# Modulation vectors of a hybrid encoder layer: VectorE's products with the condition vector taken by output channel, 2048 columns multiplied and summed in one operation, in place of 512-wide scaled additions

## The chip, the core and the metric

The kernel runs on one core of one Trainium2 chip. The metric is device microseconds from start to end of one execution. A core has five engines: TensorE (PE, matrix products into PSUM), VectorE (DVE), ScalarE (ACT), GpSimd (POOL) and SyncE (SP, which here only issues transfers). Sixteen DMA engines move data between device memory and the on-chip memory of 128 partitions.

## The reference, cut to what matters

```python
mod = jax.nn.silu(c) @ ada_w + ada_b          # c (1, 2048), ada_w (2048, 6 * 2048)
sh_m, sc_m, g_m, sh_f, sc_f, g_f = jnp.split((mod + ada_table[layer])[:, None, :], 6, axis=-1)
h = _rms(x, norm_mix_pre) * (1 + sc_m) + sh_m
y = _rwkv7_mix(h, ...)                          # 512 tokens, 2048 channels, 32 heads of 64
x = x + g_m * _rms(y, norm_mix_post)
h = _rms(x, norm_ffn_pre) * (1 + sc_f) + sh_f
f = _conv_ffn(h, ...)                           # hidden width 5504
x = x + g_f * _rms(f, norm_ffn_post)
```

Everything is float32. `silu(c) @ ada_w` is a product of one vector with a 2048 x 12288 matrix, 16 MB for each of the six modulation vectors. The change is about four of them, numbered as in the code: 2 is `g_m`, 3 is `sh_f`, 4 is `sc_f`, 5 is `g_f`.

## The kernel before, in words

Activations lie channel by token: 16 tiles of 128 channels (`KT` = 16) by 512 tokens. Every large product is taken in three matmuls of a split of both operands into a high and a low part (`mm3`, L265 to L267). Weights come in chunks of eight 128 x 128 blocks (`w_load`, L207, three buffers `wr`, on SP's queue). `w_split` halves a chunk: ACT writes the high part `wh` (L220), then VectorE the low part `wl` by a subtraction (L222), with four buffers each. So one half-chunk feeds four calls of `mm3`, which is 12 matmuls.

Each `mm3` calls `tick()`, which advances every generator in the list `sides` by one step. Work beside the products (the modulation vectors among it) is written as such generators and so is spread over the products; a number called pace says how many ticks lie between two jobs. The framework's scheduler then orders each engine's instructions by a simulation of the program; `behind()` tells it to put an operation after the last `wl`.

Vectors 0 and 1 are made by matmuls in the first stage (L361). Vectors 2 to 5 are made by `ada_jobs`. It goes over quarters of 512 output columns, and in a quarter over the 16 blocks of 128 input channels: a 128 x 512 tile of the matrix (`js`, or `xt` where six spare tiles are used) is loaded on SP (L458, 256 KB), and VectorE adds it, scaled by the 128 values of silu(c) for that block, to a running sum `ja` (L482; L477 for the first). After 16 blocks each partition holds a partial sum, so `finish` lets PE sum over the partitions by four matmuls with a column of ones (L464, which the profile counts as eight, two passes each), and VectorE adds the bias (L466). PE takes its queue in order, so what is queued behind L464 waits until the last `ja` is there.

Four stretches hold these jobs. `sc_f` (16 quarters x 16 blocks / 4 = 64 jobs) runs in the v products, with two buffers. Five of the eight quarters of `g_m` and `sh_f` run on POOL in the scan stage. The last three (48 jobs) run in the first output product `wo`, with six buffers `xt`. `g_f` (64 jobs) runs at the start of the last product `fo`, with three buffers. VectorE has 176 of the 256 jobs, or 11 of the 16 quarters.

Of the kernel before, what the change touches and what calls it, by code (L numbers as in the profile page):

```python
# [10 lines left out]
F32 = mybir.dt.float32  # L11
F32R = mybir.dt.float32r
AF = mybir.ActivationFunctionType
ALU = mybir.AluOpType

T = 512
# [14 lines left out]
         "mu0", "mu1", "mu2", "mu3", "mu4", "mu5", "w0", "a0", "kk", "ka", "rk", "lnw", "lnb", "c"]  # L31
VI = {n: i for i, n in enumerate(VEC_D)}


# [120 lines left out]
def body(ctx, tc, g, ap):  # L155
# [286 lines left out]
    QC = min(512, D)  # L442
    QB = QC // P

    def all_of(*vis):
        return [(vi, q) for vi in vis for q in range(D // QC)]

    def ada_jobs(pool, parts, bk, pace, bufs, eng=V, sums=1, get=None, last=False, to="ja"):
# [5 lines left out]
        def load(i):  # L454
            if i < len(todo):
                vi, q, k = todo[i]
                got[i] = get(i % bufs) if get else pool.tile([P, QC], F32, tag="js", name="js", bufs=bufs)
                nc.sync.dma_start(got[i], ap["ada2"][vi - 2, q, :, k])  # L458

# [35 lines left out]
        yield from finish()  # L495


    vp_stack = ExitStack()
# [27 lines left out]
    sides.append(xrest)  # L526
    jobs = ada_jobs(vp, all_of(4), 7, (1, 1, 1, 2), 2)
    vouts = [v_out(vbank[j], j) for j in range(nv0)]
# [465 lines left out]
    opened, jobs = [], []  # L994
    on_pool = len(all_of(2, 3)) * 5 // 8

    def begin():
        while fixed in sides or inv[0] in sides:
            yield
        ld_a[0], ld_b[0] = load_a(0), load_b(0)  # L1000
        for i, hv in enumerate(HV):
            nc.sync.dma_start(LH[i][hv, :, HD - i * HD:P - i * HD], d_bnd[0][hv, :, 2 - 2 * i])
        while s1_last in sides:
            yield
        invert_ready(KT)
        ss_stack.close()
        pool_of[0] = ss_stack.enter_context(tc.tile_pool(name="scn2", bufs=1))
        opened.append(True)
        wst["pool"] = 2
        ld_k[0] = load_k(0)  # L1010
        yield from solve(0)
        load_v(0, 0)
        load_v(0, 1)
        jobs.append(ada_jobs(pool_of[0], all_of(2, 3)[:on_pool], 2, (4,), 2, G, 2))
        sides.extend((s2_a, s2_b, jobs[0]))
# [66 lines left out]
    def spare(tag, name, w=T):  # L1082
        return ap_.tile([P, w], F32, tag=tag, name=name)
# [3 lines left out]
    def pair(tag, name):  # L1087
        t = ap_.tile([P, 2, T], F32, tag=tag, name=name)
        return [t[:, 0], t[:, 1]]
# [6 lines left out]
    acc1, accx = pair("b0", "acc")  # L1096
    xts = pair("b2", "xt") + pair("b3", "xt") + pair("b5", "xt")
    NX = len(xts)
    sqs = pair("b4", "osq")
# [63 lines left out]
    for b in range(KT - NL):  # L1163
        if b >= KT - NL - 4:
            fetch_x(*divmod(b - (KT - NL - 4), 2))
        ps = po[b] if b < n0 else kinner("wo", b, yx, bank((2, 6)[b % 2]))
        block_out(b, ps, acc1, yo[b], sqs[b % 2])
        if b == 1:
            jobs = ada_jobs(ap_, all_of(2, 3)[on_pool:], 7, (2,), NX, get=lambda i: xts[i], last=True, to="b1")
            sides.append(jobs)  # L1170
# [26 lines left out]
    def hidden(j, pg, pv):  # L1197
        if not units:
            units["g"], units["v"] = pair("b2", "ug"), spare("b3", "uv")
        ug = conv(pg, j, units["g"][j % 2])  # L1200
# [217 lines left out]
    ap_ = ctx.enter_context(tc.tile_pool(name="outp", bufs=1))  # L1418
    jobs = ada_jobs(ap_, all_of(5), 7, (2,), 3, last=True)
    sides.append(jobs)  # L1420
# [99 lines left out]
def layout(x):  # L1520
# [6 lines left out]
    for i, key in enumerate(g.units):  # L1527
# [9 lines left out]
    a["ada2"] = np.ascontiguousarray(  # L1537
        x["ada_w"].reshape(KT, P, 6, D // q, q)[:, :, 2:].transpose(2, 3, 1, 0, 4))
    cols = list(x["ada_b"].reshape(6, D)) + list(x["ada_table"][0].reshape(6, D))
# [23 lines left out]
```

## Time and profile before

| | us |
|---|---|
| three runs | 2730.96, 2741.63, 2741.87 (median 2741.63) |
| the profiled execution, its own time | 2733.9 |
| its span, first to last instruction | 2732.1 |
| PE busy | 2591.5 (95%) |
| VectorE busy | 2054.8 (75%) |
| ScalarE busy | 1332.1 (49%) |
| GpSimd busy | 811.5 (30%) |

The 1.8 us between the profiled execution's time and its span lie around the first and the last instruction. Busy times of engines overlap, and a busy engine is not always the one that others wait for; a row of a group gives its busy time, the mean of one instruction, and the idle time of the engine just before with what ended it.

### The profile page before, as it was taken

Reading aid. Unit: us, or ns where it says so; the run is one execution under the profiler, and the core shown is the slowest. Engines: PE = TensorE matmul, PEld = TensorE weight load, DVE = VectorE, ACT = ScalarE, POOL = GpSimd, SP = SyncE. Lnnn points to the kernel's source line nnn. Section 1 sums busy time; section 2 is a strip of 40 time slices with the busy share of each in tenths; the row PEclk is TensorE's granted clock in tenths of the full one; section 3 lists DMA queues with packets and bytes.
Section 4 is the critical chain, followed back from the end, with each engine's and each line's share of the span. In section 5 each row is a group of like instructions: output and inputs, shape, how many; then the busy total and the mean of one; then the engine's idle time right before and its main releaser. Section 6 shows DMA issues by size and latency. Waiting matters only on the chain.

```text
span 2732.1 us, 47677 instructions
## 1 busy us (share of the span) xinstructions
PE 2591.5 (95%) x17758; PEld 2277.4 (83%) x17758; DVE 2054.8 (75%) x3117; ACT 1332.1 (49%) x2313; POOL 811.5 (30%) x877
## 2 busy tenths in 40 slices
PE   5899999889999999999889999999999999999997
PEld 3568778667778787789789999999999988888896
DVE  6978588888677768668888788887888876644477
ACT  4442255454444445444665555555555553243464
POOL 3543013776878545401431111112121100000000
PEclk8999999999999999999999999999999999999998
DMA  8759776567776767477566767767767658623366
GB/s 307 281 194 347 240 252 216 193 196 237 207 175 189 198 170 195 127 269 237 187 198 195 198 194 192 205 190 201 197 192 205 175 184 283 205 94 101 99 201 206
DMA packets 301961, 555.59 MB, mean 203 GB/s; under 512 B 124352, under 2 KB 157504, under 8 KB 297632
## 3 DMA queue, kind: packets, MB, share of 16 engines
q1 hardware_dynamic: 271936, 441.05, 50.2%
q0 software_dynamic: 29360, 110.77, 15.4%
q8 instruction: 140, 2.29, 0.3%
q14 instruction: 93, 0.76, 0.1%
q10 hardware_dynamic: 432, 0.72, 0.1%
HBM read 474.18 MB, written 78.25 MB: 202 GB/s over the span
## 4 chain that ended last, share of the span: by engine, by line
PE 52%; DVE 4%; DMA 3%; issue 1%; ACT 1%; POOL 0%; DVEq 0%; ACTq 0%; POOLq 0%; SPq 0%
PE bk L1348 10%; PE bk L1347 10%; PE bk L1346 10%; PE bk L267 7%; PE bk L265 7%; PE bk L266 7%; DMA js<-ada 1%; DVE wl L222 1%; POOL acc L1137 0%; DVE fo L1443 0%; DVE yo L1128 0%; DMA x1t<-d_x 0%; PE bk L859 0%; DMA out<-x1t 0%; DVE ja L482 0%
## 5 line engine op out<-in xcount | busy, mean ns | idle before, releaser
L265 PE MATMUL bk<-xh,wh 128*128 128x512 f32 (+1 forms) x2204 | 779.1, 364 | 15.2 <-ACT wh L220 5.1
L266 PE MATMUL bk<-xl,wh 128*128 128x512 f32 (+1 forms) x2204 | 784.2, 360 | 1.9 <-DVE xl L1152 1.7
L267 PE MATMUL bk<-xh,wl 128*128 128x512 f32 (+1 forms) x2204 | 766.0, 362 | 15.7 <-DVE wl L222 15.2
L220 ACT CAST wh<-wr 128x512 fp32r<-128x512 f32 x584 | 357.5, 619 | 523.6 <-PE bk L266 446.9
L222 DVE TENSOR_TENSOR wl<-wr,wh 128x512 fp32r<-128x512 f32 x518 | 379.9, 739 | 210.5 <-ACT wh L220 191.5
L265 PEld LDWEIGHTS bk<-xh,wh 128*128 128x128 f32 x2204 | 419.8, 192 | 80.2 <-ACT wh L220 6.3
L267 PEld LDWEIGHTS bk<-xh,wl 128*128 128x128 f32 x2204 | 410.4, 192 | 83.8 <-DVE wl L222 23.2
L266 PEld LDWEIGHTS bk<-xl,wh 128*128 128x128 f32 x2204 | 421.2, 192 | 62.9 <-issue 3.0
L1297 POOL DMA_DIRECT2D ss<-w x78 | 68.0, 872 | 624.4 <-DMA ss<-w 386.1
L1347 PE MATMUL bk<-xl,wh 128*128 128x256 f32 x832 | 235.5, 283 | 0.0
L1348 PE MATMUL bk<-xh,wl 128*128 128x256 f32 x832 | 235.5, 283 | 0.0
L1346 PE MATMUL bk<-xh,wh 128*128 128x256 f32 x832 | 235.4, 283 | 0.0
L1346 PEld LDWEIGHTS bk<-xh,wh 128*128 128x128 f32 x832 | 159.7, 192 | 0.0
L1347 PEld LDWEIGHTS bk<-xl,wh 128*128 128x128 f32 x832 | 159.7, 192 | 0.0
L1348 PEld LDWEIGHTS bk<-xh,wl 128*128 128x128 f32 x832 | 159.7, 192 | 0.0
L1443 POOL TENSOR_TENSOR fo<-fo,rs 128x256 f32<-128x256 f32 x4 | 3.7, 914 | 489.3 <-ACT rs L1114 489.3
L482 DVE SCALAR_TENSOR_TENSOR ja<-js,cs,ja 128x512 f32<-128x512 f32 x120 | 89.8, 748 | 55.6 <-DMA js<-ada 54.7
L222 POOL TENSOR_TENSOR wl<-wr,wh 128x512 fp32r<-128x512 f32 x66 | 98.1, 1489 | 99.3 <-ACT wh L220 76.6
L1346 PE MATMUL bk<-xh,wx 128*128 128x256 f32 x416 | 117.7, 283 | 0.0
L1347 PE MATMUL bk<-xl,wx 128*128 128x256 f32 x416 | 117.7, 283 | 0.0
L1348 PE MATMUL bk<-xh,wx 128*128 128x256 f32 x416 | 117.7, 283 | 0.0
L1484 DVE TENSOR_TENSOR xl<-act,xh 128x512 fp32r<-128x512 f32 (+1 forms) x172 | 92.3, 552 | 27.0 <-ACT xh L1483 26.1
(302 smaller groups left out, 5962.8 us busy)
## 6 DMA issues: line engine op xcount, KB each, us to landing
wr<-w SPq DMA_DIRECT2D x370, 512.0 KB
js<-ada SPq DMA_DIRECT2D x208, 256.0 KB
ss<-w SPq DMA_DIRECT2D x78, 512.0 KB
ss<-w POOLq DMA_DIRECT2D x78, 512.0 KB, 8.2
ada<-ada SPq DMA_DIRECT2D x32, 1024.0 KB
w<-w SPq DMA_DIRECT2D x39, 512.0 KB
d_bnd<-bnd POOLq DMA_DIRECT2D x16, 768.0 KB, 4.1
d_gs<-big POOLq DMA_DIRECT2D x16, 768.0 KB, 4.6
```

Of the source, the lines that this page charges most:

```text
L220: S.copy(hi, r)
L222: ins = on.tensor_tensor(lo, r, hi.bitcast(F32), ALU.subtract)
L265: PE.matmul(out[:, cs], wh[0:kp, 0:m], xh[0:kp, cs], start=start, stop=False)
L266: PE.matmul(out[:, cs], wh[0:kp, 0:m], xl[0:kp, cs], start=False, stop=False)
L267: PE.matmul(out[:, cs], wl[0:kp, 0:m], xh[0:kp, cs], start=False, stop=stop)
L482: eng.scalar_tensor_tensor(a, w, c, a, ALU.mult, ALU.add)
L1297: G.dma_start(t[:, i], chunk(j, other), accum_op=ALU.add)
L1346: PE.matmul(ps, wh, xh, start=start and k == 0, stop=False, skip_group_check=True)
L1347: PE.matmul(ps, wh, xl, start=False, stop=False, skip_group_check=True)
L1348: PE.matmul(ps, wl, xh, start=False, stop=k == CH - 1, skip_group_check=True)
L1443: prev[of[kt]] = of[kt].tensor_tensor(fo[kt][:, cs], fo[kt][:, cs], rs4[:, cs], ALU.mult)
L1484: V.tensor_tensor(ahl[e][1][:, cs], act[f][:, cs], ahl[e][0][:, cs].bitcast(F32), ALU.subtract)
```

## The change

For VectorE's 11 quarters the matrix is laid out the other way: a tile `js` has 128 output channels on the partitions and the 2048 input channels along a row. silu(c) is written to device memory once (`d_c`) and read back as a row `crow` that is the same on all partitions. One operation multiplies the tile with that row and sums each partition's 2048 products into one column of `part`; a second one adds the bias. PE's sums are no longer needed for these quarters; POOL's five quarters stay as they were. 44 blocks of 128 channels take the place of 11 quarters: 16 for `sc_f`, 12 for `sh_f`, 16 for `g_f`. The last 16 are taken in two passes of 1024 columns, 32 operations, the second pass adding to the first's result. Buffers of `js`: two everywhere (1 MB each; 512 KB for `g_f`). Paces: 9 ticks a job for `sc_f`, 8 for `sh_f`, 5 for `g_f`.

```diff
-                nc.sync.dma_start(got[i], ap["ada2"][vi - 2, q, :, k])
+                nc.sync.dma_start(got[i], ap["ada2"][(vi - 2) * (D // QC) + q, :, k])
...
+    d_c = dram("d_c", (KT, P))
+    part = cp.tile([P, KT], F32, name="part")
+    def c_row(t, cols=slice(0, D)):
+        n = cols.stop - cols.start
+        nc.sync.dma_start(t, d_c.rearrange("k p -> (k p)")[cols].unsqueeze(0).to_broadcast([P, n]))
+        return t
+    def row_jobs(todo, crow, get, bufs, pace, cols=slice(0, D)):
+        got = {}
+        def load(i):
+            if i < len(todo):
+                got[i] = get(i % bufs)
+                nc.sync.dma_start(got[i], ap["ada3"][ROWS.index(todo[i])][:, cols])
+        for i in range(bufs):
+            load(i)
+        yield
+        for n, (vi, b) in enumerate(todo):
+            w, to = got.pop(n), part[:, b:b + 1]
+            with behind():
+                V.scalar_tensor_tensor(w, w, 1.0, crow, ALU.mult, ALU.mult, accum_out=to)
+            V.tensor_tensor(mods[vi][:, b:b + 1], to, mods[vi][:, b:b + 1] if cols.start else bt[:, vi, b:b + 1], ALU.add)
+            load(n + bufs)
+            for _ in range(pace):
+                yield
...
-    jobs = ada_jobs(vp, all_of(4), 7, (1, 1, 1, 2), 2)
+    nc.sync.dma_start(d_c.rearrange("k p -> p k"), cs)
+    crow = c_row(vp.tile([P, D], F32, name="crow"))
+    jobs = row_jobs([r for r in ROWS if r[0] == 4], crow, lambda i: vp.tile([P, D], F32, tag="js", name="js", bufs=2), 2, 9)
...
-            jobs = ada_jobs(ap_, all_of(2, 3)[on_pool:], 7, (2,), NX, get=lambda i: xts[i], last=True, to="b1")
+            jobs = row_jobs([r for r in ROWS if r[0] < 4], c_row(spare("b2", "crow", D)),
+                            lambda i: tp.tile([P, D], F32, tag=f"t3{'hl'[i]}", name="js"), 2, 8)
...
-            units["g"], units["v"] = pair("b2", "ug"), spare("b3", "uv")
+            t = ap_.tile([P, 4, T], F32, tag="b2", name="ug")
+            units["g"], units["v"] = [t[:, 0], t[:, 1]], t[:, 2]
...
-    jobs = ada_jobs(ap_, all_of(5), 7, (2,), 3, last=True)
+    def in_halves():
+        for cols in (slice(0, D // 2), slice(D // 2, D)):
+            row = c_row(ap_.tile([P, D // 2], F32, tag="crow", name="crow"), cols)
+            yield from row_jobs([r for r in ROWS if r[0] == 5], row,
+                                lambda i: ap_.tile([P, D // 2], F32, tag="js", name="js", bufs=2), 2, 5, cols)
+    jobs = in_halves()
...
+    a["ada3"] = np.ascontiguousarray(np.stack([x["ada_w"][:, vi * D + b * P:vi * D + (b + 1) * P].T for vi, b in row_blocks(D)]))
```

The lines move by 11 and more, so L222 of before is L233 of the changed kernel, L265 is L276, L207 is L218, L508 is L551. The first place is PE's queue at the end of the v products (`bk` is a bank of PSUM; L508 turns a block of v). Before:

```order
L266 MATMUL bk_3002<-xl,wh 128x512
L508 MATMUL bk_3013<-cst,vs 128x128 x4
L464 MATMUL bk_2730<-ones,ja 128x1 x4
L265 MATMUL bk_3003<-xh,wh 128x512
L266 MATMUL bk_3003<-xl,wh 128x512
```

and now:

```order
L277 MATMUL bk_2849<-xl,wh 128x512
L551 MATMUL bk_2860<-cst,vs 128x128 x4
L276 MATMUL bk_2850<-xh,wh 128x512
L277 MATMUL bk_2850<-xl,wh 128x512
L278 MATMUL bk_2850<-xh,wl 128x512
```

The four sums with `ones` are gone, and the products of the last two v blocks follow the turned block directly.

The second place is VectorE's queue in the `wo` stretch (L1107, now L1149, adds squares for a norm). Before, from one quarter's last additions to the next one's first:

```order
L482 SCALAR_TENSOR_TENSOR ja<-xt,cs,ja 128x512 x2
L222 TENSOR_TENSOR wl<-wr,wh 128x512 x3
L1107 TENSOR_TENSOR acc<-acc,osq 128x512
L222 TENSOR_TENSOR wl<-wr,wh 128x512
L477 TENSOR_SCALAR ja<-xt,cs 128x512
L466 TENSOR_TENSOR mod_87<-bk_11839,bt 128x4
L482 SCALAR_TENSOR_TENSOR ja<-xt,cs,ja 128x512 x3
L222 TENSOR_TENSOR wl<-wr,wh 128x512
L482 SCALAR_TENSOR_TENSOR ja<-xt,cs,ja 128x512 x2
```

and now, from the first of the twelve blocks on:

```order
L534 SCALAR_TENSOR_TENSOR js,part<-js,crow 128x2048 x2
L233 TENSOR_TENSOR wl<-wr,wh 128x512
L535 TENSOR_TENSOR mod_87<-part,bt 128x1
L233 TENSOR_TENSOR wl<-wr,wh 128x512
L535 TENSOR_TENSOR mod_87<-part,bt 128x1
L233 TENSOR_TENSOR wl<-wr,wh 128x512
L534 SCALAR_TENSOR_TENSOR js,part<-js,crow 128x2048
L1149 TENSOR_TENSOR acc<-acc,osq 128x512
L233 TENSOR_TENSOR wl<-wr,wh 128x512
```

One long operation stands where four to six short ones stood, with one or two `wl` between two of them. Between the first and the last long operation VectorE has, beside them: in the v products 34 `wl`, 20 of L521, 9 of L510 and 8 of L518; in the `wo` stretch 19 `wl` and 4 of L1107; in the `fo` stretch 39 `wl` and 35 `xl` (L1484).

The third place is SP's queue at the start of the `wo` stretch (`xin` is the layer's input, read again). Before:

```order
L207 DMA wr<-w 128x1024 x6
L1161 DMA xin<-xT 128x8x256 x4
L207 DMA wr<-w 128x1024 x2
L458 DMA xt<-ada 128x512 x8
L207 DMA wr<-w 128x1024
```

and now:

```order
L218 DMA wr<-w 128x1024 x6
L526 DMA js<-ada 128x2048 x2
L1203 DMA xin<-xT 128x8x256 x4
L218 DMA wr<-w 128x1024 x2
L516 DMA crow<-d_c 128x2048
L218 DMA wr<-w 128x1024 x2
L526 DMA js<-ada 128x2048 x2
```

Two 1 MB tiles now go ahead of `xin` and of two weight chunks, and the 1 MB row `crow` ahead of the next two. The write of `d_c` (2048 elements of 4 bytes) stands early in the first stage, behind the first three weight chunks and ahead of the fourth tile of vectors 0 and 1.

## Rows read from the trace of the kernel before

**Rows 1.** The page: span, and TensorE's busy time

```profile
span 2732.1 us, 47677 instructions
PE 2591.5 (95%) x17758; PEld 2277.4 (83%) x17758; DVE 2054.8 (75%) x3117; ACT 1332.1 (49%) x2313; POOL 811.5 (30%) x877
```

**Rows 2.** Busy time by stretch: v products, after a wait, `wo`, `fo`

```profile
core 0: us, PE busy (x) PEld busy (x) DVE busy (x) ACT busy (x) POOL busy (x), PEclk, DMA share, GB/s
200.00:260.00 60.00, 59.89 (x293) 50.27 (x292) 54.30 (x87) 15.18 (x26) 24.07 (x42) 1.00 0.98 353
260.00:327.00 67.00, 63.49 (x308) 53.13 (x306) 38.02 (x59) 14.86 (x25) 7.08 (x11) 1.00 0.75 253
327.00:332.00 5.00, 4.69 (x18) 3.98 (x19) 2.49 (x6) 1.68 (x3) 0.76 (x1) 0.66 0.89 308
1185.00:1260.00 75.00, 75.00 (x432) 66.34 (x431) 61.46 (x97) 32.10 (x61) 0.00 (x0) 1.00 0.86 293
2232.00:2375.00 143.00, 139.46 (x617) 115.09 (x618) 102.28 (x161) 54.66 (x92) 0.00 (x0) 0.98 0.82 281
```

**Rows 3.** Groups by line: the matmuls with ones

```profile
L464 PE MATMUL bk<-ones,ja 128*128 128x1 f32 x128 | 16.6, 241 | 6.1 <-DVE ja L482 5.6 <-DVE bv L849 0.4
```

**Rows 4.** TensorE in order of time, around one sum in the v products

```profile
start us, us, engine line op out<-in xcount [idle before <-releaser]
...
253.16 0.39 PE L265 MATMUL bk<-xh,wh 128*128 128x512 f32 x1
253.39 0.39 PE L266 MATMUL bk<-xl,wh 128*128 128x512 f32 x1
253.89 1.05 PE L464 MATMUL bk<-ones,ja 128*128 128x1 f32 x8
254.80 0.47 PE L267 MATMUL bk<-xh,wl 128*128 128x512 f32 x1
```

**Rows 5.** The same at the end of the v products

```profile
327.31 1.25 PE L464 MATMUL bk<-ones,ja 128*128 128x1 f32 x8 [3.82 <-DVE ja L482]
328.42 0.77 PE L265 MATMUL bk<-xh,wh 128*128 128x512 f32 x1
...
331.51 0.39 PE L266 MATMUL bk<-xl,wh 128*128 128x512 f32 x1
```

**Rows 6.** The same in the `fo` stretch

```profile
2344.11 0.39 PE L266 MATMUL bk<-xl,wh 128*128 128x512 f32 x1
2345.44 1.02 PE L464 MATMUL bk<-ones,ja 128*128 128x1 f32 x8 [0.95 <-DVE ja L482]
2346.33 0.48 PE L267 MATMUL bk<-xh,wl 128*128 128x512 f32 x1
```

**Rows 7.** VectorE's groups by line, shapes apart

```profile
L482 DVE SCALAR_TENSOR_TENSOR ja<-js,cs,ja 128x512 f32<-128x512 f32 x120 | 89.8, 748 | 55.6 <-DMA js<-ada 54.7
L1303 DVE TENSOR_TENSOR s<-ss,w 128x1024 f32<-128x1024 f32 x39 | 47.7, 1222 | 0.8
L663 DVE TENSOR_TENSOR_SCAN cs<-cst,sw 128x512 f32<-128x512 f32 x16 | 21.0, 1313 | 0.3
L374 DVE TENSOR_TENSOR shm<-bk,bt 128x1 f32<-128x1 f32 x16 | 2.4, 148 | 8.4 <-PE bk L373 8.4
```

**Rows 8.** VectorE in order of time, v products: two `wl`, then one L482

```profile
316.67 1.29 DVE L222 TENSOR_TENSOR wl<-wr,wh 128x512 fp32r<-128x512 f32 x2
317.89 0.75 DVE L482 SCALAR_TENSOR_TENSOR ja<-js,cs,ja 128x512 f32<-128x512 f32 x1
318.56 0.68 DVE L510 COPY vt<-bk 128x512 f32<-128x512 f32 x1
```

**Rows 9.** Waits: engine, line, waited for: total us, times, longest

```profile
ACT wh L220 <- PE bk L266: 446.9, 320, 4.7
...
PE bk L267 <- DVE wl L222: 15.2, 24, 1.9
```

**Rows 10.** SP in order of time at the start of the `wo` stretch

```profile
1170.68 5.29 SPq L1161 DMA_DIRECT2D xin<-xT  x4
1176.07 7.05 SPq L207 DMA_DIRECT2D wr<-w  x2
1184.32 6.38 SPq L458 DMA_DIRECT2D xt<-ada  x8
```

**Rows 11.** The page: the queue of SP's transfers, packets, MB, share of 16 engines

```profile
q1 hardware_dynamic: 271936, 441.05, 50.2%
```

**Rows 12.** Busy time by stretch early in the first stage

```profile
35.00:40.00 5.00, 3.84 (x9) 2.90 (x10) 3.00 (x4) 0.70 (x2) 0.56 (x1) 0.50 0.35 118
40.00:45.00 5.00, 4.68 (x34) 3.09 (x33) 0.26 (x3) 0.99 (x2) 0.12 (x1) 0.87 0.16 26
```

More of the change, by code (lines that the diff above doesn't have):

```diff
@@ L32, with on_pool, row_blocks @@
 VI = {n: i for i, n in enumerate(VEC_D)}
+def on_pool(d):
+    return d // min(512, d) * 2 * 5 // 8
+def row_blocks(d):
+    n = min(512, d) // P
+    return [(vi, b) for vi in range(2, 6) for b in range(d // P) if ((vi - 2) * (d // P) + b) // n >= on_pool(d)]
 class Cfg:
@@ L443, in body @@
     QB = QC // P
+    ROWS = row_blocks(D)
     def all_of(*vis):
@@ L994, in body @@
     opened, jobs = [], []
-    on_pool = len(all_of(2, 3)) * 5 // 8
     def begin():
@@ L1013, in begin @@
         load_v(0, 1)
-        jobs.append(ada_jobs(pool_of[0], all_of(2, 3)[:on_pool], 2, (4,), 2, G, 2))
+        jobs.append(ada_jobs(pool_of[0], [(g // (D // QC) + 2, g % (D // QC)) for g in range(on_pool(D))], 2, (4,), 2, G, 2))
         sides.extend((s2_a, s2_b, jobs[0]))
@@ L1096, in body @@
     acc1, accx = pair("b0", "acc")
-    xts = pair("b2", "xt") + pair("b3", "xt") + pair("b5", "xt")
-    NX = len(xts)
     sqs = pair("b4", "osq")
@@ L1537, in layout @@
     a["ada2"] = np.ascontiguousarray(
-        x["ada_w"].reshape(KT, P, 6, D // q, q)[:, :, 2:].transpose(2, 3, 1, 0, 4))
+        x["ada_w"].reshape(KT, P, 6, D // q, q)[:, :, 2:].transpose(2, 3, 1, 0, 4).reshape(-1, P, KT, q)[:on_pool(D)])
+    a["ada3"] = np.ascontiguousarray(np.stack([x["ada_w"][:, vi * D + b * P:vi * D + (b + 1) * P].T for vi, b in row_blocks(D)]))
     cols = list(x["ada_b"].reshape(6, D)) + list(x["ada_table"][0].reshape(6, D))
```

## The prediction

> **What bounds the kernel now.** I read the page first, then the busy times of the stretches in which the jobs run, then TensorE's timeline around each of its sums, and last VectorE's groups and the waits. On the page PE is busy for 2591.5 us of a span of 2732.1 [rows 1]. By stretch the reader is to see that PE is the bound just where the changed work lies: 59.89 of 60 us and 63.49 of 67 in the v products, 75.00 of 75 in `wo`, 139.46 of 143 in `fo` [rows 2]. There a microsecond taken from PE's queue is a microsecond off the end, and one taken from VectorE is worth nothing unless PE waits for it. VectorE is busy for 54.30 of 60 us, 38.02 of 67, 61.46 of 75 and 102.28 of 143: behind PE, but not far. PE waits for `wl` for 15.2 us in 24 pieces over the whole kernel, and ACT waits for PE 320 times before it can write the next `wh` [rows 9]: the split weights are ready early, and the four buffers hold it back. One matmul of 512 columns starts every 0.23 us [rows 4], so a half-chunk of 12 lasts 2.73 us, and two half-chunks ahead, about 5.5 us, is the delay of VectorE that PE does not feel.
>
> **What the change removes.** All gain must come from PE's sums with ones. The group has 128 instructions and 16.6 us of busy time [rows 3]; 11 of 16 quarters go, so 88 x 16.6 / 128 = 11.4 us. One sum in the timeline bears this out: matmuls start at 253.39 and, with the eight between, at 254.80, which is 1.41 us in place of 0.23 [rows 4]. With them go PE's waits for the last `ja`, 5.6 us [rows 3]: 3.82 at the end of the v products [rows 5], 0.95 in `fo` [rows 6], and the rest in one more like it. Behind the wait of 3.82 us PE is also slow: seven matmuls start from 328.42 to 331.51, 3.09 us in place of 7 x 0.23 = 1.6 [rows 5], and the granted clock of that stretch is 0.66 [rows 2], a mean between the two levels of 1.2 and 2.4 GHz. That is another 1.5 us. Sum: 11.4 + 5.6 + 1.5 = 18.5 us. The products and the splits behind the sums are next in line and were ready, so nothing takes the place of the waits on PE itself.
>
> **What it costs VectorE.** Off go 165 of L482 at 0.748 us [rows 7] and 11 first products. On come 28 operations of 2048 columns, 32 of 1024, and 60 additions of one column, 0.148 us each by the nearest row (L374) [rows 7]. The trace has no product with a running sum. Lower bound: from 748 ns at 512 columns to 1222 at 1024 (L1303) is 0.93 ns a column, so 748 + 1536 x 0.93 = 2.17 us at 2048. An upper bound is a scan, in which each column needs the one before: 1.313 us for 512 columns, 5.25 for 2048 [rows 7]. I take 2.3 us, and 1.3 for 1024: the operation is that of L482, with as many streams, and only the sum is new. Reading out the sum, 0.1 to 0.15 us by L374, comes on top. Total 28 x 2.55 + 32 x 1.55 = 121 us, about what went (165 x 0.748 = 123). So VectorE is not relieved, and only the grain changes.
>
> Whether that grain hurts follows from what stands between the long operations. In a row one `wl` takes 0.61 us (two in 1.22, from 316.67 to 317.89) and an operation like L482 0.67 [rows 8]. V products: 34 `wl` last 34 x 2.73 = 93 us on PE; VectorE needs 51 x 0.61 + 20 x 0.67 + 16 x 2.45 = 84. `wo`: 52 us on PE, 23 x 0.61 + 12 x 2.45 = 43 on VectorE. `fo`: 106 us, 74 x 0.61 + 32 x 1.45 = 92. Each fits, with 9 to 14 us over. A single long operation, even two in a row (4.9 us), stays under the 5.5 us that the splits are ahead. I put 0 here; the other end is in the second rival.
>
> **What it costs the queues.** (a) Writing `d_c`: 2048 elements of 4 bytes, 128 for each DMA engine. SP's packets take 0.502 x 16 x 2732.1 / 271936 = 81 ns each on average [rows 11], which makes 10 us at most and a little at least. It stands ahead of the fourth tile of vectors 0 and 1; behind that the DMA engines are only 0.35 and 0.16 busy from 35 to 45 us [rows 12], which is room. I take 2 us. (b) At the start of `wo` 2 MB of `js` go ahead of `xin` and the next weights; at 353 GB/s [rows 2] that is 6 us. These weights are issued from 1176 to 1183 [rows 10], two chunks (10.9 us) ahead of their use; hidden, but then little is left. Behind that, 12 tiles of 1 MB in 52 us are 242 GB/s, and weights (512 KB in 5.46 us) 96: 338 of the 353 that the busiest stretch reached. With two buffers, not six, a late tile is a late VectorE at once. I take 2 us, and 0 to 12 as bounds (1 us for each tile). (c) In `fo` the second half of `crow` can be loaded only when the 16th product is through, and the 17th waits for it: 512 KB at 353 GB/s, 1.5 us, and the way there; VectorE stands still some 3 us, inside the 5.5. I take 1 us. (d) At the end of the v products the row tiles are done before the products are, where the old jobs ran on behind the wait of [rows 5]; the transfers there get easier. I take 1 us of gain.
>
> Sum: 18.5 + 1 - 2 - 2 - 1 = 14.5 us. The profiled execution's 2733.9 less 14.5 is 2719.4. The median of the three runs is 7.7 us above that execution and the lowest 2.9 below, so it lies in their midst rather than at their median; I add 2.5 us and forecast 2722.
>
> **A rule against the change.** L482 reads two float32 tiles from on-chip memory and takes 748 ns for 512 columns, where an operation of 1024 takes 1222 [rows 7]; nothing is halved there. The Trainium skill, Vector Engine (DVE) Microarchitecture Reference, section Points that are easy to get wrong, says that this instruction "with two non-bf16 SBUF sources halves throughput", since both read ports are taken and none is left for reading the accumulator back. By that rule L482 would be slow already, and it is not; whether it holds once the sum is asked for no run here shows yet. By the rule the sum would be that of the second rival.
>
> **The rivals.** First, the loads: two buffers of 1 MB do not keep pace in `wo`, nor those of 512 KB in `fo`. For it speaks that VectorE waited 54.7 us for `js` with two and three buffers [rows 7] and that the room is 338 of 353 GB/s; against it that PE did not wait for `wl` in those stretches. A tile 1 us late each time makes 12 us in `wo`, less 5.5: 6.5 us, and some 4 in `fo`. Time 2722 + 10 = 2732.
>
> Second, and on the other side: the running sum costs a second cycle a column, as in the scan, whose 1.313 us is 1.76 times L482. The operation then takes 4.0 to 5.25 us, say 4.5, and 2.3 for 1024. V products: 44.5 + 16 x 4.5 = 116 against 93, 23 late, less 5.5: 18. `wo`: 14 + 54 = 68 against 52: 10. `fo`: 45 + 32 x 2.45 = 123 against 106: 12. Together 40 us more, so 2762. It decides from about 4.0 us an operation on, where what is late beyond the 5.5 (v products 10 us, `wo` 4.5, `fo` 0) eats the 14.5. Against it: L482's own rate.
>
> Third, the change does not do what it says: the sums go, but PE stands elsewhere for the same time, since the next splits or the start (the write of `d_c` at its 10 us, and another order of the first stages) are as late. Time 2736.
>
> **How the numbers follow.** Chances: forecast 0.52, loads 0.22, second cycle 0.12, third 0.14. A measurement of this kernel can tell about 0.5% from no change, 13.7 us of 2741.63; below 2727.9 is faster. The forecast's own range is 2706 (all 18.5, nothing lost, and some 9 from another order) to 2730. Faster: most of the forecast and a little of the loads, 0.48. Slower, above 2755.3: the second cycle and a little of the third, 0.14. Same: 0.38. The range from 2705 to 2758 takes in the first and third rival and leaves out most of the second.
>
> **What would show it.** In the profile of the changed kernel: 40 of L464 left in place of 128 (6 us less 0.4 of busy time); no wait near 327 us; the operation of 2048 columns at about 2.3 us; PE's waits for `wl` still near 15 us. Wrong it would be if that operation took over 4.0 us, if VectorE waited for `js` or `crow` and PE for `wl` in `wo` or `fo`, or if the first stage ended later than before.

## The result: 0.73% slower

The changed kernel takes 2752.9 us (median of 20 runs, 2742.9 to 2758.5), the kernel before 2733.4 in the same runs. The ratio is 1.0073, with a 95% interval of 1.0062 to 1.0083. The forecast of 2722 is 31 us too low and on the wrong side; the range held the time.

The page of the changed kernel, against [rows 1]: the span is 16.3 us longer, and PE is busy for 6.3 us less.

```profile
span 2748.4 us, 47108 instructions
PE 2585.2 (94%) x17670; PEld 2263.7 (82%) x17670; DVE 2033.9 (74%) x3110; ACT 1329.8 (48%) x2313; POOL 810.1 (29%) x877
```

What was said of the operations themselves came out. These are VectorE's groups for the new lines, shapes kept apart (busy time, mean ns of one, idle time before and what ended it), which answer to [rows 7]:

```profile
L534 DVE SCALAR_TENSOR_TENSOR js<-js,crow 128x2048 f32<-128x2048 f32 x28 | 64.0, 2288 | 5.7 <-DMA js<-ada 4.6 <-DMA crow<-d_c 1.1
L534 DVE SCALAR_TENSOR_TENSOR js<-js,crow 128x1024 f32<-128x1024 f32 x32 | 39.1, 1224 | 22.0 <-DMA js<-ada 17.6 <-DMA crow<-d_c 4.4
L535 DVE TENSOR_TENSOR mod<-part,bt 128x1 f32<-128x1 f32 x44 | 6.8, 155 | 0.1
L534 DVE DVE_READ_ACCUMULATOR js<-js,crow 128x1 f32 x60 | 5.0, 84 | 0.0
```

The reader is to see 2.29 us for 2048 columns and 1.22 for 1024, each followed by a second instruction of 84 ns that reads out the sum. Of PE's sums 40 are left, as forecast, the first at 863.8 us, so none stands in the v products any more ([rows 3]):

```profile
L476 PE MATMUL bk<-ones,ja x40: 166/250/271, 863.8 to 1198.4; 128*128 128x1 f32 x40
```

In the v products PE is now busy without a gap to 320 us, where [rows 2] had 63.49 of 67 from 260 us on; `wo` and `fo`, moved by the 14 us that the kernel is late there, lose 1.0 us against 75.00 of 75 and 4.4 us against 139.46 of 143. Busy time by stretch (PE, weight loads, VectorE, ScalarE, GpSimd, granted clock, DMA share, GB/s):

```profile
200.00:260.00 60.00, 60.00 (x290) 50.57 (x289) 52.20 (x80) 16.44 (x28) 20.17 (x34) 1.00 1.02 404
260.00:320.00 60.00, 60.00 (x286) 50.40 (x285) 44.45 (x65) 14.85 (x25) 11.35 (x19) 1.00 0.90 324
1199.00:1274.00 75.00, 74.01 (x419) 65.14 (x418) 57.35 (x83) 32.75 (x61) 0.00 (x0) 1.00 0.84 305
2246.00:2389.00 143.00, 135.02 (x571) 109.29 (x572) 98.42 (x188) 53.77 (x91) 0.00 (x0) 0.97 0.81 286
```

PE's waits (us in total, times, longest), which answer to [rows 9]: those for VectorE's `wl` grew from 15.2 to 21.7 us, and 9.9 us for a `wl` made by POOL are new.

```profile
PE bk L278 <- DVE wl L233: 21.7, 26, 2.9
...
PE bk L278 <- POOL wl L233: 9.9, 5, 3.9
```

**Where the time went.** To compare two traces stage by stage I numbered the 4,516 products (calls of `mm3`, and the like calls of the FFN) by the start of their first matmul. The table has the time from one mark to the next; its other rows are the experiments below, from one profiled execution each. The column "scan" runs from the 325th to the 950th product: the keys, the receptance products and the scan over the tokens, up to the first `wo` products. It holds no changed operation.

| us | to 113th (start) | 113-325 (v products) | 325-950 (scan) | 950-1400 (`wo`) | 3690-3860 (`fo`) |
|---|---|---|---|---|---|
| before | 184.0 | 169.2 | 805.9 | 231.4 | 121.6 |
| changed kernel | 186.1 | 158.6 | 828.8 | 232.3 | 124.9 |
| write_only | 188.0 | 165.9 | 796.2 | 231.3 | 120.2 |
| wo_only | 187.2 | 173.0 | 805.1 | 229.4 | 120.5 |
| fo_only | 187.1 | 164.9 | 799.6 | 233.9 | 124.6 |
| v_only | 187.3 | 159.0 | 826.4 | 233.4 | 127.4 |
| v_pace8 | 186.2 | 162.5 | 803.6 | 233.9 | 120.3 |
| v_split_dve | 187.2 | 158.8 | 801.3 | 232.7 | 120.0 |
| write_split_dve | 189.3 | 169.4 | 822.0 | 233.8 | 120.6 |
| write_nopool | 187.4 | 168.2 | 782.9 | 230.5 | 119.4 |
| v_nopool | 187.8 | 158.8 | 781.0 | 231.9 | 119.6 |
| v_noload | 186.4 | 158.7 | 827.8 | 232.7 | 120.8 |
| split_noload | 188.0 | 171.2 | 830.0 | 233.9 | 121.9 |
| v_js_pool | 185.1 | 158.8 | 825.5 | 233.9 | 119.7 |
| split_js_pool | 189.0 | 167.6 | 821.0 | 233.4 | 121.5 |
| v_wo_scan_dve | 186.9 | 159.3 | 814.1 | 230.8 | 121.7 |
| v_wo_split | 191.8 | 158.7 | 811.6 | 235.3 | 119.4 |
| all_split_dve | 189.8 | 159.3 | 801.2 | 231.4 | 124.1 |
| all_three | 186.6 | 158.5 | 800.7 | 230.4 | 129.6 |
| fo_three | 186.7 | 167.5 | 798.9 | 231.5 | 129.3 |

By these two executions the changed kernel wins 10.6 us in the v products, where the gain was expected, and loses 22.9 us in the scan, where nothing was changed but the order in which the scheduler put the instructions.

### The profile page after: what moved, and what is told of

It reads as the page before. It is cut to its first block, busy times and chain, and to the rows that moved or that the text cites. A ratio compares the mean times of both kernels' runs of the same rounds, so it can differ in the third digit from the quotient of the medians.

```text
span 2748.4 us, 47108 instructions
## 1 busy us (share of the span) xinstructions
PE 2585.2 (94%) x17670; PEld 2263.7 (82%) x17670; DVE 2033.9 (74%) x3110; ACT 1329.8 (48%) x2313; POOL 810.1 (29%) x877
## 4 chain that ended last, share of the span: by engine, by line
PE 53%; DMA 9%; DVE 6%; POOL 4%; issue 3%; SPq 1%; ACT 1%; DVEq 0%; POOLq 0%; ACTq 0%
PE bk L1392 10%; PE bk L1391 10%; PE bk L1390 10%; PE bk L278 7%; PE bk L276 7%; PE bk L277 7%; DMA js<-ada 4%; DVE wl L233 1%; POOL js L491 1%; POOL ja L492 1%; DMA wr<-w 1%; PE bk L904 1%; DMA x1t<-d_x 1%; DMA tt<-d_tt 1%; DMA out<-x1t 1%
## 5 line engine op out<-in xcount | busy, mean ns | idle before, releaser
L276 PE MATMUL bk<-xh,wh 128*128 128x512 f32 (+1 forms) x2204 | 784.3, 366 | 21.0 <-ACT wh L231 5.9
L278 PE MATMUL bk<-xh,wl 128*128 128x512 f32 (+1 forms) x2204 | 767.8, 363 | 32.2 <-DVE wl L233 21.7
L233 DVE TENSOR_TENSOR wl<-wr,wh 128x512 fp32r<-128x512 f32 x518 | 381.9, 743 | 249.8 <-ACT wh L231 229.3
L276 PEld LDWEIGHTS bk<-xh,wh 128*128 128x128 f32 x2204 | 421.2, 193 | 85.1 <-ACT wh L231 7.1
L233 POOL TENSOR_TENSOR wl<-wr,wh 128x512 fp32r<-128x512 f32 x66 | 101.0, 1534 | 96.1 <-ACT wh L231 96.0
L534 DVE SCALAR_TENSOR_TENSOR js<-js,crow 128x1024 f32<-128x1024 f32 (+1 forms) x60 | 103.1, 1720 | 27.7 <-DMA js<-ada 22.2
```

What stands on the lines that cost most here:

```text
L233: ins = on.tensor_tensor(lo, r, hi.bitcast(F32), ALU.subtract)
L276: PE.matmul(out[:, cs], wh[0:kp, 0:m], xh[0:kp, cs], start=start, stop=False)
L278: PE.matmul(out[:, cs], wl[0:kp, 0:m], xh[0:kp, cs], start=False, stop=stop)
L534: V.scalar_tensor_tensor(w, w, 1.0, crow, ALU.mult, ALU.mult, accum_out=to)
```

## The experiments

All kernels start from the changed one and take parts of it back. Each ratio is to the kernel before in runs on the same chip, with its 95% interval.

### Which part costs

write_only has rows nowhere and keeps the write of `d_c`; v_only has them in the v products alone, wo_only and fo_only in `wo` and in `fo` alone. For the v products the edit is this, and in `wo` and `fo` likewise:

```diff
-    crow = c_row(vp.tile([P, D], F32, name="crow"))
-    jobs = row_jobs([r for r in ROWS if r[0] == 4], crow, ..., 2, 9)
+    jobs = ada_jobs(vp, all_of(4), 7, (1, 1, 1, 2), 2)
```

> The kernel before with the write of d_c alone added on SP's queue (nothing reads it; all 16 quarters made as before). Theory A (the loss came with the new order of the scan stage, and that order came with the row products in the v products): the order here is nearly that of before, so the time is that of before within 4 us (ratio 0.9985 to 1.0015). Theory B (the write of d_c at its start delays and reorders the first stage, and the scan stage inherits it): here too the scan stage ends 14 us or more late, ratio 1.005 or more.

> Rows of 2048 columns in the v products alone (sc_f); the wo and fo stretches as before. Theory A: PE is about 10 us ahead of before by the end of the v products, and 14 us behind at the start of wo, with the loss of some 25 us between 980 and 1160 us; from there nothing changes, so the time is that of before plus 13 to 16 us, ratio 1.005 to 1.006. Rival (the loss came from the rows in wo and fo, and the scan stage's loss in the one profile was a matter of that execution): faster than before by about 10 us, ratio 0.996.

> Rows of 2048 columns in the wo stretch alone (twelve blocks of g_m and sh_f); v products and fo as before; d_c is written at the start. Theory A: the three quarters' sums were 24 x 16.6 / 128 = 3.1 us, of which the changed kernel kept about 1 us, so 0 to 3 us faster than the write alone, ratio to before 0.9985 to 1.0005. Rival of the prediction (loads of 1 MB in two buffers don't keep pace): 6.5 us or more slower, ratio 1.002 or more, with PE waiting for wl in that stretch.

> Rows of two passes of 1024 columns in the fo stretch alone (g_f); v products and wo as before; d_c is written at the start. Theory A: the second half of crow is loaded only when the first pass is through, VectorE stands still for 4 us or more and PE behind it; the changed kernel lost 6 us there and won 5.2 us (32 sums' 4.2 us and a wait of 0.95) around it, so 0 to 3 us slower than the write alone, ratio 1.000 to 1.0015. The prediction's own numbers: 1 us lost at the switch, 5 us won, so 4 us faster, ratio 0.9985.

Measured: write_only 0.9993 (0.9973 to 1.0013), v_only 1.0071 (1.0046 to 1.0096), wo_only 0.9990 (0.9970 to 1.0010), fo_only 1.0002 (0.9984 to 1.0019). The whole loss is in v_only, and its table row has the whole change's two figures: 159.0 us in the v products, 826.4 in the scan. Theory B falls: the write of `d_c` alone moves the start by 4.0 us here (by some 3 over all kernels that have it) and leaves the scan at 796. The four kernels that keep before's jobs in the v products and the `wl` where they were (write_only, wo_only, fo_only, fo_three) have scans of 796 to 805; that spread of 9 us is what one execution differs from another, and the 20 us above it are not. The rows of just this stretch show what differs, first before, then write_only, then v_only (the stretch and its length, PE, weight loads, VectorE, ScalarE, GpSimd, granted clock, DMA share, GB/s):

```profile
353.20:1159.07 805.87, 764.87 (x5270) 617.19 (x5269) 618.17 (x940) 393.83 (x687) 476.79 (x530) 0.97 0.65 195
353.86:1150.06 796.20, 757.01 (x5271) 609.93 (x5269) 625.58 (x940) 394.28 (x687) 479.29 (x531) 0.98 0.67 197
346.30:1172.68 826.38, 762.86 (x5262) 612.12 (x5261) 610.99 (x930) 392.07 (x686) 474.44 (x532) 0.97 0.64 188
```

PE stands still for 41.0 us in before and 39.2 in write_only, nearly the same; what parts these two is PE's busy time for the same matmuls, 7.9 us more at a granted clock of 0.97 than at 0.98 (means over the stretch of its two levels, 1.2 and 2.4 GHz). In v_only PE is busy for about as long as in before and stands for 63.5 us. So the loss against before is idle time of PE.

That the order differs is seen in the traces, where VectorE's instructions of this stretch can be compared one by one with instance numbers left out. The 939 of before stand in the same sequence in write_only; the longest sequence that before and v_only have in common is 659. The 929 of v_only are, in their sequence, those of the changed kernel.

In `fo` fo_only and the changed kernel agree, 124.6 and 124.9 us against 119 to 122 with the old jobs: the rows lose 3 to 5 us there. (v_only's 127.4, with the old jobs, stands alone; v_noload and v_js_pool, which have the same jobs there, take 120.8 and 119.7. In v_only's execution the granted clock of this stretch is 0.97, where before's is 1.00, and PE stands for 3.9 us in place of 1.8; why is not known.) VectorE's queue and SP's in the changed kernel at the switch from one half of `crow` to the other (start, us, idle time before and its end):

```profile
2325.11 1.23 DVE L534 SCALAR_TENSOR_TENSOR js<-js,crow 128x1024 f32<-128x1024 f32 x1 [0.47 <-DMA js<-ada]
...
2326.37 0.33 SPq L516 DMA_DIRECT2D crow<-d_c  x1
...
2326.93 1.29 DVE L233 TENSOR_TENSOR wl<-wr,wh 128x512 fp32r<-128x512 f32 x2
...
2332.59 1.23 DVE L534 SCALAR_TENSOR_TENSOR js<-js,crow 128x1024 f32<-128x1024 f32 x1 [4.37 <-DMA crow<-d_c]
```

`crow` is issued only when the last product of the first half is through, and takes 6.2 us to its first use, 4.37 of them with VectorE idle. VectorE waits for `js` beside this, but not longer in total than it did with three buffers of the old jobs (2225 to 2420 us, before; the changed kernel has 17.6 us, in the second row of its groups above):

```profile
L482 DVE SCALAR_TENSOR_TENSOR ja<-js,cs,ja 128x512 f32<-128x512 f32 x60 | 44.9, 748 | 17.4 <-DMA js<-ada 16.8
```

In before PE waits for no `wl` in these 195 us. In the changed kernel it does, five times, and all five lie behind the switch, from 2336 to 2380 us:

```profile
PE bk L278 <- DVE wl L233: 5.6, 5, 2.9
```

### Is it POOL, or the order as such

In the scan the chain of work that ended last in v_only runs, at several places, from a load through POOL's products to a `wl` on POOL and then to PE. From 873 to 888 us (start, us, what):

```profile
873.00 4.34 DMA js<-ada
...
879.44 1.24 POOL ja L492
...
885.42 0.70 POOL js L491
...
886.41 1.29 POOL wl L233
...
887.74 0.50 PE bk L278
```

Theory C made this the cause. Theory D held that any other order can cost or gain, and POOL's `wl` is one sign of it. PE's waits that end with a `wl` of POOL come to 6.3 us, while PE stands 22.5 us more in v_only's scan than in before's (640 to 1175 us: us in total, times, longest):

```profile
PE bk L278 <- POOL wl L233: 6.3, 4, 3.6
```

The first line goes for v_split_dve (no `wl` of the scan on POOL), the next two change for v_nopool and write_nopool (POOL's 80 products left out, with rows in the v products and without), the last two for v_pace8:

```diff
-        wst["pool"] = 2
...
-        sides.extend((s2_a, s2_b, jobs[0]))
+        sides.extend((s2_a, s2_b))
...
-    jobs = row_jobs(..., crow, ..., 2, 9)
+    jobs = row_jobs(..., crow, ..., 2, 8)
```

> As v_only, but every low part wl of the scan stage is made by VectorE, none by POOL (a POOL wl stands behind POOL's products, which wait for their tile js). Theory C (in the order that v_only got, POOL's late wl hold PE's queue, and the scan's chain behind it, up in the scan stage): the 4 us waits for POOL's wl go, the scan stage loses under 10 us instead of 25, and the time comes to 2738 or less, ratio 1.002 or less. Theory D (what counts is that the scan stage's whole order became another one, with the filling products early and the chain late, and POOL is only one place where that shows): the time is that of v_only, ratio 1.004 or more, or anything, since this too is another order.

> As v_only, but POOL's 80 products with c in the scan stage are left out (five of the eight quarters of g_m and sh_f are set to zero); the rest as in v_only. Theory C: without those products and their loads POOL's wl are never late, and the row products' gain of 10 us in the v products stays: 8 us or more faster than the same kernel without row products. Theory D: still slower than that kernel, by 10 us or more, or by an amount that has nothing to do with POOL.

> As write_only (all quarters of VectorE made as before), but POOL's 80 products in the scan stage are left out (the same five quarters set to zero): the reference point for v_nopool. Both theories: faster than before by 5 to 25 us, since POOL's loads and waits leave the scan stage.

> As v_only, with 8 ticks between two row products in the v products in place of 9. The work is the same, the scheduler's order of the scan stage becomes another one. Theory D: the gain of 7 to 11 us by the end of the v products is there as in v_only, and the scan stage comes out by chance, anywhere from 10 us faster to 30 us slower than before; a time under 2735 would show that row products do not need to cost the scan stage anything. Rival (row products in the v products always bring the scan stage 25 us): ratio 1.006 to 1.008 as in v_only.

Measured: v_split_dve 0.9970 (0.9946 to 0.9993), v_pace8 0.9980 (0.9960 to 1.0000), v_nopool 0.9878 (0.9845 to 0.9910), write_nopool 0.9926 (0.9896 to 0.9956). So the rows in the v products need not cost the scan anything: with a pace of 8, the same work in another order, the scan takes 803.6 us in place of 826.4, though the v products take 162.5 and keep only part of the gain. Without POOL's products both orders have the same scan, 781.0 and 782.9, and the kernel with rows is 13.4 us faster by the medians (2701.5 and 2714.9), 9.4 of it in the v products of the table. PE's busy time in the scan, the same stretch as in the rows of before and v_only above, shows the same. First v_pace8, then v_nopool:

```profile
348.69:1152.28 803.59, 755.18 (x5263) 607.86 (x5262) 605.10 (x925) 392.61 (x683) 474.62 (x530) 0.98 0.65 191
346.62:1127.67 781.05, 748.57 (x5239) 602.89 (x5237) 573.29 (x926) 393.87 (x686) 276.41 (x376) 0.99 0.57 172
```

PE stands for 48.4 us with a pace of 8 and for 32.5 without POOL's products, against 63.5 in v_only. The rest of what v_nopool wins over v_only is PE's busy time, 14 us less, with the sums of POOL's quarters left out and at a granted clock of 0.99 in place of 0.97.

### A control, and the repairs

write_split_dve is write_only without the first line here, all_split_dve the whole change without it. The rest is for fo_three (fo_only in three passes) and all_three (all_split_dve with it); `nxt` is loaded first with the first part:

```diff
-        wst["pool"] = 2
...
-        for cols in (slice(0, D // 2), slice(D // 2, D)):
-            row = c_row(ap_.tile([P, D // 2], F32, tag="crow", name="crow"), cols)
+        for k, cols in enumerate([slice(0, 768), slice(768, 1536), slice(1536, 2048)]):
+            row = nxt
+            if k < 2:
+                nxt = c_row(cut(k + 1, "crow"), parts[k + 1])
...
-            yield from row_jobs([r for r in ROWS if r[0] == 5], row,
-                                lambda i: ap_.tile([P, D // 2], F32, tag="js", name="js", bufs=2), 2, 5, cols)
+            yield from row_jobs([r for r in ROWS if r[0] == 5], row, lambda i: cut(k, "js"), 2, 3, cols)
```

So the pace changes too, from 5 ticks to 3, for 48 products in place of 32, and the two buffers of `js` hold less.

> The control of v_split_dve: write_only (all products of VectorE made as before) with every wl of the scan stage on VectorE. Theory C: before had no wait of PE for POOL's wl in the scan stage, so nothing is won by moving them; VectorE gets 36 operations of 0.61 us more; time that of before within 6 us, ratio 0.998 to 1.002, and v_split_dve stays 6 to 12 us faster than this. Theory D (any other order): no forecast, -10 to +30 us.

> The whole change (rows in v products, wo and fo) with every wl of the scan stage on VectorE. Theory C: v_split_dve's gain, wo's 1 to 2 us on top, and nothing from fo, where the switch of crow eats the gain: 0 to 3 us under v_split_dve's 2722.5, so 2719 to 2724, ratio 0.996 to 0.9975; PE waits nowhere for POOL's wl.

> As fo_only, but in three passes of 768, 768 and 512 columns with two buffers of crow, so that the next pass's crow is loaded a pass ahead; js stays at two buffers (of 768 columns). Theory (the 6 us at the switch are VectorE's wait for crow, which can only be loaded when the first pass has let go of it): the wait for crow goes, fo ends 3 to 5 us ahead of fo_only, ratio to before 0.9975 to 0.9995. Rival (the time at the switch is the loads of js, which start anew with each pass, or VectorE's own time, which grows by 16 operations): no better than fo_only, and with two switches perhaps worse, ratio 1.000 or more.

> The whole change with both repairs: every wl of the scan stage on VectorE, and fo in three passes with crow a pass ahead. If both theories hold: 3 to 5 us under all_split_dve, 2715 to 2720, ratio 0.9945 to 0.9965, faster than both kernels.

Measured: write_split_dve 1.0082 (1.0052 to 1.0113), all_split_dve 1.0001 (0.9981 to 1.0021), fo_three 1.0043 (1.0027 to 1.0058), all_three 1.0017 (0.9998 to 1.0036). The control breaks theory C as the general cause. The same edit, which moves the same operations from POOL to VectorE, brought v_only back by 30 us and costs the order of before 22 us: the scan goes from 826.4 to 801.3 in the one and from 796.2 to 822.0 in the other, and in the control no `wl` of POOL can be at fault. (The control's profiled execution took 2761.3 us, 8 above the median, so 822.0 may be high by some us.) PE's longest sums of waits in its scan are spread over loads and VectorE:

```profile
PE bk L834 <- DMA tt<-d_tt: 8.5, 8, 2.9
PE bk L903 <- DVE qz L904: 6.2, 6, 1.9
PE bk L851 <- DVE qz L904: 3.6, 3, 2.1
PE bk L934 <- DVE sv L930: 3.3, 4, 1.8
```

all_split_dve, the whole change with that edit, comes out level with the kernel before and not below it as expected; `fo` takes 124.1 us in it and 120.0 in v_split_dve. The repair of `fo` failed, and all_three with it. In fo_three VectorE no longer waits for `crow` at all, but for `js` more than before (fo_only first, then fo_three):

```profile
L534 DVE SCALAR_TENSOR_TENSOR js<-js,crow 128x1024 f32<-128x1024 f32 x32 | 39.1, 1223 | 22.1 <-DMA js<-ada 18.1 <-DMA crow<-d_c 4.0
```

```profile
L534 DVE SCALAR_TENSOR_TENSOR js<-js,crow 128x768 f32<-128x768 f32 x32 | 30.6, 956 | 19.2 <-DMA js<-ada 19.1
L534 DVE SCALAR_TENSOR_TENSOR js<-js,crow 128x512 f32<-128x512 f32 x16 | 11.1, 692 | 11.7 <-DMA js<-ada 11.7
```

30.9 us of idle time took the place of 22.1, VectorE's products of `fo` themselves grew from 39.1 to 41.7 us with 16 more sums to read out and to add, and `fo` went from 124.6 to 129.3 us. PE's waits for `wl` there, 2225 to 2420 us, became more and shorter (fo_only first, then fo_three):

```profile
PE bk L278 <- DVE wl L233: 5.4, 4, 2.9
```

```profile
PE bk L278 <- DVE wl L233: 8.8, 10, 1.6
```

Whether the smaller buffers, the pace or the 16 more operations cost most was not tried apart.

### Loads or POOL's time

Since the scan was short in both orders without POOL's products, their loads were suspected next: theory E, SP's one queue, in which a tile for POOL waits for POOL and the scan's own loads wait behind it. Theory F was POOL's time.

v_noload and split_noload start from v_only and write_split_dve and load only the first two tiles; v_js_pool and split_js_pool start from the same two and load POOL's tiles on POOL's own queue:

```diff
+                if eng is G and i >= bufs:
+                    got[i] = first[i % bufs]
+                    return
...
-                nc.sync.dma_start(got[i], ap["ada2"][...])
+                dma = G.dma_start if eng is G else nc.sync.dma_start
+                dma(got[i], ap["ada2"][...])
```

> As v_only (costly order), but POOL's 80 products in the scan stage read the first two tiles again and again: 78 of the 80 loads of js in that stage are left out, and with them the sense of five quarters; POOL's work stays. Theory E (the loads on SP's queue are what costs): the stage from the 325th to the 950th product comes from 826 to 790 us or less, near the 781 without POOL's products; time 2715 or less. Theory F (POOL's time itself): 815 us or more, time 2740 or more.

> As write_split_dve (the other costly order, without row products), with the same 78 loads left out. Theory E: the stage comes from 822 to 795 us or less, time 2725 or less. Theory F: 815 us or more, time 2745 or more.

> As v_only, with POOL's tiles js loaded by POOL's own queue and not SP's: the traffic stays, SP no longer waits for POOL, and POOL spends some 0.6 us more on each of 80 loads. Theory E in the narrow form (SP's queue stands and the scan's loads behind it): the stage comes from 826 to 805 us or less, time 2732 or less. Theory E in the wide form (the traffic itself delays the scan's loads) or theory F: 815 us or more.

> As write_split_dve, with POOL's tiles js loaded by POOL's own queue. Narrow form of theory E: the stage comes from 822 to 805 us or less, time 2735 or less. Otherwise 815 us or more.

Measured: 1.0066 (1.0044 to 1.0088), 1.0074 (1.0036 to 1.0111), 1.0065 (1.0047 to 1.0082) and 1.0104 (1.0078 to 1.0131), with scans of 827.8, 830.0, 825.5 and 821.0. Theory E falls in both forms: without 78 of the 80 loads the scan is as long as with them. What is left of the two is theory F, which the next kernel tries. One reservation: each of these kernels again has an order of its own (of v_only's 929 operations of VectorE in the scan, v_noload shares a sequence of 867 and v_js_pool one of 811).

### POOL's products on VectorE

v_wo_scan_dve has rows in the v products and `wo`, and this edit; v_wo_split has the same rows and no `wl` of the scan on POOL:

```diff
-        jobs.append(ada_jobs(pool_of[0], [...], 2, (4,), 2, G, 2))
+        jobs.append(ada_jobs(pool_of[0], [...], 2, (4,), 2, V, 2))
```

> Rows in the v products and in wo, fo as before, and the 80 products of the scan stage on VectorE instead of POOL (one operation of 0.75 us each where POOL takes two, 2.5 us together). Theory G (POOL's products cost by holding up VectorE's operations that take two inputs from on-chip memory, and the order decides which): ri and wl come near their lengths without POOL's products (0.75 us, against 1.19 and 1.01 in v_only), VectorE gets 60 us more of work but loses some 40 us of holding, and the stage from the 325th to the 950th product comes from 826 to 800 us or less; time 2722 or less. Rival (VectorE, at 70% of the scan stage already, becomes what the scan's chain waits for): 815 us or more, time 2740 or more, with ri still short.

> Rows in the v products and in wo, fo as before, every wl of the scan stage on VectorE (the order of v_split_dve up to wo). v_split_dve gave 0.997; the rows in wo give 1 to 2 us more: 2719 to 2723, ratio 0.9955 to 0.9975, faster than both kernels. If wo's rows gain nothing: 0.997 again.

Measured: v_wo_scan_dve 1.0010 (0.9998 to 1.0022), v_wo_split 0.9986 (0.9972 to 1.0000). Theory G was right about the durations and wrong about what they are worth. `ri` multiplies two tiles of on-chip memory (the shortest, median and longest of 32 in ns), in v_only, v_nopool and v_wo_scan_dve:

```profile
L874 DVE TENSOR_TENSOR ri<-rsb,E x32: 673/862/6187, 652.5 to 1105.6; 64x512 f32<-64x512 f32 x32
```

```profile
L874 DVE TENSOR_TENSOR ri<-rsb,E x32: 673/689/1490, 654.6 to 1062.3; 64x512 f32<-64x512 f32 x32
```

```profile
L874 DVE TENSOR_TENSOR ri<-rsb,E x32: 671/689/1687, 652.4 to 1090.2; 64x512 f32<-64x512 f32 x32
```

With POOL's products gone from POOL, VectorE's operations are short again, and yet the scan takes 814.1 us, between 800 and the 815 that the rival asked for: what VectorE won it spent on the products, and it is busy for 623.5 us of the stretch where it was for 611.0 in v_only. So theory F does not hold as POOL's time alone either: the 80 products cost the scan some 14 to 48 us over the 782 without them, on whichever engine, and how much goes by the order. v_wo_split is no better than v_split_dve, so the rows in `wo` add nothing that can be measured. Its 811.6 us in the scan, in an execution 9 us above its median, stand beside 801 in three kernels where VectorE has the very same sequence there (v_split_dve, all_split_dve, all_three), which shows once more what executions differ by. The best kernel of the study that leaves nothing out is v_split_dve, 30 us under the changed one and at 0.9970 of the one before, which is less than the 0.5% that the prediction called a difference.

## Why the prediction was wrong

**The gain** was right in place and size. Of the 18.5 us the v products were to bring 4.2 (32 of the 128 sums) + 3.8 + 1.5, and 1 from (d): 10.5. Measured are 10.6 in the changed kernel; over the kernels with rows at a pace of 9 the stretch takes 158.5 to 159.3 us, and 164.9 to 173.0 where the old jobs stand, so a gain of 6 to 14: that the two figures agree to 0.1 is luck.

**VectorE's cost** was right: 2.29 + 0.08 + 0.16 = 2.53 us a row, forecast 2.55. The second rival did not happen: no operation came near its 4.5 us, and 1024 columns take 1224 ns with the sum, where a product of 1024 columns without one took 1222 (L1303, [rows 7]). The Trainium skill, Vector Engine (DVE) Microarchitecture Reference, Points that are easy to get wrong, says that this instruction loses half its throughput with two sources in on-chip memory that are not bf16. The trace does not agree with that rule here, neither at 2048 columns nor at 1024, though both sources are float32 and the sum is asked for.

**(a)** The write of `d_c`: 2 us forecast, some 3 measured (start of the 113th product at 184.0 us in the one execution of before, 185.1 to 191.8 in the kernels with the write). **(b)** `wo`: 3.1 us and a wait were to be won and 2 lost; the columns differ by no more than executions do, and wo_only's 0.9990 does not tell it from nothing. **(c)** `fo`: this was mis-sized. VectorE was to stand still for 3 us inside the cover of 5.5, at a cost of 1, beside 5.2 us won; it stands for 4.4 at the switch, and behind it PE, which waited for no `wl` here before, waits for 5.6 us in five pieces. The sum took the cover as full when the switch came; a reading that no run tests is that the waits for `js` (17.6 us in all, 16.8 before) draw on it too. The stretch became 3 us longer in place of 4 shorter. Two signs that the prediction named for its being wrong came with (a) and (c), the first stage that ended later and PE's waits for `wl` in `fo`, but neither is the main loss.

**The step that failed** is the one that had no term. The sum added what the changed stretches win and lose, and the sentence that the forecast's own range has "some 9 from another order" was all that the 625 products between the v products and `wo` were given. Their order changed with the rows, and it cost 22.9 us in the profiles, twice the gain: PE stands 63.5 us there in v_only in place of 41.0, with the same products to make. The third rival, that the change "doesn't do what it says" since PE stands elsewhere for the same time, names the outcome, but placed it in the next splits and the start, and gave it 2736. What the runs showed in its place: v_only has the whole loss, v_pace8 has the same rows and part of the gain (162.5 us in the v products) without the loss, and write_split_dve has a loss of that size without the rows. The loss belongs to the order of the scan and not to the row products.

**The base.** The 0.5% that the prediction called a difference was taken from 2741.63, the median of three runs; over twenty the kernel before takes 2733.4, and 0.5% above that is 2747.1. By this measure 2752.9 is slower, to which the prediction gave 0.14.

**What stays open** is which pairs of instructions make an order costly. Shown is that of five orders with POOL's products and loads as they were three (those of before, v_pace8 and v_split_dve, with what shares them) take 796 to 812 us and two (v_only with the changed kernel, and write_split_dve) 822 to 829, that both orders tried without POOL's products lie at 781 to 783, and that neither the loads nor POOL's `wl` are the one cause. Of the orders that were compared only those of v_only and v_pace8 make the same products with the same split of work between the engines; the others move work too, and the kernel before was not run at another pace. Argued, not shown, is the rest: PE's queue holds filling products and the scan's dependent chain in one sequence, and each late operation of another engine holds up both.

## What to carry to other kernels

Where a scheduler orders the whole program, an edit in one stage is also a new order for the later ones, and a price for that belongs in the sum and in the range: here 25 us, more than the gain. Before blaming or praising the edit, run it with a neutral change of pace and run the kernel before with one: v_pace8 took 25 us off, and write_split_dve, which is less neutral, put 22 on the kernel before. Count a cover once for all waits that draw on it: in `fo` VectorE's wait at the switch was 4.4 us, under the 5.5 of cover, and PE waited all the same.

## What the runs showed of the hardware

In these traces VectorE's operations with two inputs from on-chip memory are held up while POOL works, and those that read PSUM are not. From 640 to 1175 us, first in v_only, then in v_nopool (`wl` has two inputs from on-chip memory, `qz` reads a bank of PSUM):

```profile
L233 DVE TENSOR_TENSOR wl<-wr,wh 128x512 fp32r<-128x512 f32 x47 | 47.2, 1008 | 29.4 <-ACT wh L231 25.8 <-PE bk L278 3.3
L905 DVE TENSOR_TENSOR qz<-bk,cst 128x512 f32<-128x512 f32 x64 | 42.4, 684 | 24.3 <-PE bk L935 23.9
```

```profile
L233 DVE TENSOR_TENSOR wl<-wr,wh 128x512 fp32r<-128x512 f32 x63 | 47.1, 749 | 33.7 <-ACT wh L231 26.7 <-PE bk L278 6.5
L905 DVE TENSOR_TENSOR qz<-bk,cst 128x512 f32<-128x512 f32 x64 | 43.5, 689 | 29.8 <-PE bk L935 16.2 <-PE bk L904 13.1
```

`wl` takes 1008 ns beside POOL's products and 749 without, `qz` 684 and 689. The single operations of v_only part the two cases: the 27 `wl` of these 535 us that run at the same time as some operation of POOL take 1233 ns in mean and up to 4327, the other 19 take 687 and never over 693, while `qz` takes 684 in either case. One `ri` was held for over 5 us (6187 ns against 673), from 737.3 to 743.5 us, and POOL went through eight operations in that time.

The Trainium skill, SBUF — State Buffer, section SBUF: two separate sides, says that VectorE and GpSimd share a pair of ports as an exclusive lock, which an operation of VectorE with two inputs from on-chip memory needs while GpSimd's reads that memory, and which the loser waits for in full. These rows agree with it.
